# Seven products in two more down projections, with the weights' sums made in memory by GpSimd's transfers

## The chip, the core and the metric

One core of one Trainium2 chip runs the whole program. The metric is the device time of one execution in microseconds; the median of several runs is given. TensorE multiplies (with weight loads beside), VectorE (DVE) and ScalarE (ACT) do elementwise work, GpSimd (POOL) some more of it, and SyncE (SP) issues the transfers.

## What is computed

One decoder layer on 576 tokens (512 of a prompt, 64 of samples), width 1024: a token mixer (gated linear attention and retention, four heads each), cross attention into a memory of 256 tokens, and a squared-ReLU MLP with 4096 hidden columns. Around each stands a pair of RMS norms. The part that the change touches, and the norms at the start:

```python
def rmsnorm(x, g):
    xf = x.astype(jnp.float32)
    y = xf * lax.rsqrt(jnp.mean(xf * xf, axis=-1, keepdims=True) + EPS)
    return (y * g.astype(jnp.float32)).astype(x.dtype)
...
    m, s_gla_new, s_ret_new = mixer_block(rmsnorm(x, g_pre_mix), ...)
    x = x + rmsnorm(m, g_post_mix)
    x = x + rmsnorm(cross_attn(rmsnorm(x, g_pre_xa), mem_k, mem_v, w_xq, w_xo), g_post_xa)
    hf = rmsnorm(x, g_pre_ffn)
    x = x + rmsnorm(jnp.square(jax.nn.relu(hf @ w_up)) @ w_down, g_post_ffn)
```

## The kernel before

**Products.** Activations lie transposed, columns of the model on partitions, 576 tokens in two halves of NH = 288. Every product of float32 is made of three matmuls of a faster type (fp32r), high by high, low by high, high by low (`mm3`, lines 251 to 253). So each operand is split into two tiles: ScalarE casts the high part (line 93) and VectorE subtracts it for the low part (line 94). `gemm_m` makes 128 columns by 576 tokens over the inner dimension of 1024 from one tile of weights.

**Weights.** A list `plan` holds all weight tiles in the order of use. `wfetch` has SP load the next one (512 KB) into one of six ring buffers `wraw` (line 180), `wsplit` splits it, `wnext` hands the pair on and keeps loads and splits ahead.

**MLP.** The hidden columns come in four groups g of 1024. Group 0 is made plainly, 384 matmuls up and 384 down. The hidden columns of groups 1 to 3 are made by `sevenfold`: a 2 x 2 block product (halves of the inner dimension and of the columns, with the tokens' halves) from seven products instead of eight, A11, S1, S2, A12, S3, S4 and A22, each 12 matmuls, in four blocks b; S1 to S4 multiply sums of blocks. The activations' sums are made once (`sums_f`, in `fsh`, `fsl`), and the weights' sums by VectorE, four subtractions of 512 columns a block (`minus`, line 213, in `begin`). In the down projection groups 1 and 2 are plain: eight calls of `gemm_m`, added into `y3`. The last group's down projection is the end of the kernel.

**What sets the order.** The code is written in one stream; `side` holds generators of work that `tick` advances between products, and a scheduler of the language then orders the instructions of each engine, by its own estimates of when operands are there. Each engine runs its list in order.

**The start.** SP loads the memory `mf`, the first weights `in_w_xk`, and the two halves of x (`xf`). TensorE makes the keys of the memory from its unnormalized columns and the norm is applied behind. For a norm, VectorE and ScalarE add squares up (`sq`, `ss`, `mss`, lines 349 to 353, last sum line 322), TensorE adds over partitions (line 324), VectorE scales (`ms`, line 326), GpSimd raises to the power -1/2 (`rs`, line 333), VectorE puts it on a diagonal (`dg`, line 335) and TensorE spreads it (line 342). Then VectorE scales x to `xn`, ScalarE casts `xh`, and GpSimd subtracts for `xl` (line 98). `mst` (line 415) are the memory's keys on their way out.

**The mixer.** Eight units (head, branch) of about 60 us follow from 68 us on; GpSimd makes their head norms' `rs` (line 874), which TensorE's transposes (line 1016) wait for by way of VectorE.

Of the kernel before, what the change touches and what calls it, by code (L numbers as in the profile page):

```python
# [13 lines left out]
P = 128  # L14
KT = 8
# [43 lines left out]
def decoder_step(ctx, tc, xT, memT, ktc, vc, s_gla, s_ret, w_in, w_ga, w_a2, w_mix, w_xq, w_xk, w_xv, w_xo,  # L59
                 w_up, w_ups, w_down, vecs, cst, gam, y_out, mk_out, mv_out, sg_p, sr_p, sg_s, sr_s):  # L60
# [102 lines left out]
    def seven(w, b0):  # L163
        return [(w[b0 + b][:, kh], SEVEN) for b in range(4) for kh in range(2)]
# [18 lines left out]
    def wsplit():
        if units:
            units.pop(0)()
        elif raws:
            if raws[0][1] == SEVEN:
                begin()
                return
# [4 lines left out]
            pool = staying[-1] if mode == STAY else wp  # L194
            wh = pool.tile([P, 1024], F32R, name="wh")
            wl = pool.tile([P, 1024], F32R, name="wl")
            split(wh, wl, raw)
            ready.append((wh, wl))

    def halves(w):  # L200
        return w.rearrange("p (q n) -> p q n", q=2)

    def begin():


        while len(raws) < 2:
            wfetch()
        p0, p1 = (raws.pop(0)[0] for _ in range(2))
        t = wp.tile([P, 1024], F32, name="wraw", bufs=N_RAW)
        q0, q1, qt = halves(p0), halves(p1), halves(t)  # L210

        def minus(out, a, b):
            nc.vector.tensor_tensor(out=out, in0=a, in1=b, op=ALU.subtract)

        def ring(raw):
            wh = wp.tile([P, 1024], F32R, name="wh")
            wl = wp.tile([P, 1024], F32R, name="wl")
            split(wh, wl, raw)
            ready.append((wh, wl))

        def own(raw, o, n):
            w = wq[0][:, o:o + n], wq[0][:, o + n:o + 2 * n]
            split(*w, raw)
            ready.append(w)

        def unit_a():
            ring(p0)
            wfetch()

        units.extend([unit_a, lambda: ring(t), lambda: own(p1, 0, 1024),  # L230
                      lambda: minus(q1[:, 0], q1[:, 0], qt[:, 0]), lambda: own(q1[:, 0], 2048, 512)])
# [41 lines left out]
    def sevenfold(x, p1, p5, u2, c11, c22, c12, c21):  # L273
# [374 lines left out]
    xnp = ctx.enter_context(tc.tile_pool(name="xnp", bufs=2))  # L648
# [4 lines left out]
    def add(out, a, b, op=ALU.add):  # L653
        nc.vector.tensor_tensor(out=out, in0=a, in1=b, op=op)  # L654

    def sums_f():

        for j in range(4):
# [5 lines left out]
            add(c2[:, 1], c2[:, 0], c2[:, 1])  # L664
            add(c2[:, 0], c1[:, 0], c2[:, 0], ALU.subtract)
            add(c1[:, 0], c2[:, 1], c1[:, 0], ALU.subtract)
            add(c1[:, 1], c1[:, 1], c1[:, 0], ALU.subtract)
            yield
            split(fsh[:, 2:4, j], fsl[:, 2:4, j], c2)
            split(fsh[:, 0:2, j], fsl[:, 0:2, j], c1)  # L670
            yield

    FQ = {"A11": (fh, fl, 0), "A12": (fh, fl, 1), "A22": (fh, fl, 3),
# [748 lines left out]
```

## Time and profile before

| | us |
|---|---|
| median of 3 runs | 1200.71 (1199.32 to 1202.62) |
| the profiled execution, whole | 1199.37 |
| its span in the trace | 1197.6 |
| start until the mixer's first product | 67.6 |
| mixer, cross attention | 68 to 572, 572 to 806 |
| MLP and last norm | 806 to 1197.6 |

The page gives for each engine how long it was busy in the span. The tables of stretches give the same for parts of it, with the clock that TensorE was granted and the share of time in which the 16 transfer engines were busy. In the groups by line, "busy, mean ns of one | idle before, releaser" says how long such instructions took and what the engine had waited for just before them. A timeline's row is: start, duration, engine, line, operation, output <- inputs, shape; in brackets the idle time ahead and who ended it.

### The profile page before, as it was taken

The numbers are of one execution on the slowest core, as the hardware profiler recorded it, in microseconds if no ns is written. First come the engines' busy times: TensorE is split into PE (matmuls) and PEld (weight loads), VectorE is DVE, ScalarE is ACT, GpSimd is POOL, SyncE is SP. The second block draws the span as 40 slices with busy tenths as digits, with TensorE's granted clock in tenths as the row PEclk, the third lists the DMA queues.
The fourth block names the chain that finished last, engine by engine and source line by source line (L and its number), as shares of the span: only waits on it lengthen the run. The fifth ranks groups of instructions, "written<-read, shape, count | busy, mean of one in ns | idle before, by whom it ended". The sixth has DMA issues, their size and how long they took to land.

```text
span 1197.6 us, 21977 instructions
## 1 busy us (share of the span) xinstructions
PE 1168.7 (98%) x9006; PEld 1137.6 (95%) x9006; DVE 746.6 (62%) x1332; ACT 563.3 (47%) x992; POOL 155.1 (13%) x165
## 2 busy tenths in 40 slices
PE   8899999999999999999999999999999999999995
PEld 8899999999999999999999878989999999999995
DVE  6745757465747565757868545686937546456565
ACT  5534546442445244524555434566527416515652
POOL 0522213122312222221001000000000000000000
PEclk9899999999999999999999999999999999999998
DMA  8772424242324332322644677753223223321631
GB/s 290 228 244 79 129 79 128 72 144 72 127 89 128 89 128 79 121 88 93 213 134 138 215 260 232 235 177 123 88 71 107 88 71 105 107 71 57 215 110 60
DMA packets 65621, 158.37 MB, mean 132 GB/s; under 512 B 5648, under 2 KB 34448, under 8 KB 65392
## 3 DMA queue, kind: packets, MB, share of 16 engines
q1 hardware_dynamic: 65520, 156.96, 41.0%
q8 instruction: 71, 1.16, 0.4%
q14 instruction: 30, 0.25, 0.1%
HBM read 140.68 MB, written 16.25 MB: 131 GB/s over the span
## 4 chain that ended last, share of the span: by engine, by line
PE 90%; DVE 4%; DMA 3%; issue 1%; POOL 1%; ACT 1%; SPq 0%; POOLq 0%; DVEq 0%; ACTq 0%
PE psg L251 22%; PE psg L252 22%; PE psg L253 22%; PE psa L281 6%; PE psg L281 3%; PE psa L251 2%; PE pso L281 2%; PE psa L252 1%; PE psa L253 1%; PE pso L1241 1%; DMA xf<-in_xT 1%; PE psa L1084 1%; DVE wl L94 1%; PE pso L1079 1%; DVE res L526 1%
## 5 line engine op out<-in xcount | busy, mean ns | idle before, releaser
L251 PE MATMUL psg<-xh,wh 128*128 128x288 f32 x1296 | 385.5, 298 | 0.0
L252 PE MATMUL psg<-xh,wl 128*128 128x288 f32 x1296 | 381.9, 295 | 0.8 <-DVE wl L94 0.8
L253 PE MATMUL psg<-xl,wh 128*128 128x288 f32 x1296 | 381.9, 295 | 0.0
L94 DVE TENSOR_TENSOR wl<-wraw,wh 128x1024 fp32r<-128x1024 f32 x197 | 243.4, 1236 | 89.3 <-ACT wh L93 88.5
L93 ACT CAST wh<-wraw 128x1024 fp32r<-128x1024 f32 x197 | 207.0, 1051 | 187.6 <-PE psg L253 108.2
L251 PEld LDWEIGHTS psg<-xh,wh 128*128 128x128 f32 x1296 | 243.2, 188 | 2.2 <-issue 0.8
L252 PEld LDWEIGHTS psg<-xh,wl 128*128 128x128 f32 x1296 | 243.3, 188 | 1.1 <-DVE wl L94 1.0
L253 PEld LDWEIGHTS psg<-xl,wh 128*128 128x128 f32 x1296 | 243.1, 188 | 0.1
L251 PE MATMUL psg<-hh,wh 128*128 128x288 f32 x512 | 151.2, 296 | 0.7 <-DVE y L760 0.6
L252 PE MATMUL psg<-hh,wl 128*128 128x288 f32 x512 | 151.0, 295 | 0.3 <-DVE wl L94 0.3
L253 PE MATMUL psg<-hl,wh 128*128 128x288 f32 x512 | 151.0, 295 | 0.0
L251 PEld LDWEIGHTS psg<-hh,wh 128*128 128x128 f32 x512 | 96.2, 188 | 1.6 <-issue 1.1
L252 PEld LDWEIGHTS psg<-hh,wl 128*128 128x128 f32 x512 | 96.1, 188 | 0.6 <-DVE wl L94 0.6
L253 PEld LDWEIGHTS psg<-hl,wh 128*128 128x128 f32 x512 | 96.2, 188 | 0.0
L333 POOL TENSOR_TENSOR rs<-ms,mhalf 96x3 f32<-96x3 f32 (+1 forms) x11 | 11.0, 998 | 521.5 <-DVE ms L326 521.5
L942 ACT COPY vt<-psg 128x512 f32<-128x512 f32 x16 | 9.4, 586 | 77.8 <-PE psg L253 77.8
L874 POOL TENSOR_TENSOR rs<-mv,mhalf 128x1 f32<-128x1 f32 x48 | 29.7, 619 | 112.7 <-DVE mv L869 64.6
L944 DVE COPY vd<-psg 128x128 f32<-128x128 f32 x32 | 7.8, 285 | 55.8 <-ACT vt L942 55.8
L251 PE MATMUL psg<-bh,wh 128*128 128x288 f32 x128 | 38.4, 300 | 1.6 <-ACT wh L93 1.1
L654 DVE TENSOR_TENSOR y<-psg,y 128x576 f32<-128x576 f32 x16 | 12.1, 756 | 44.2 <-PE psg L253 44.2
L252 PE MATMUL psg<-fh,wl 128*128 128x288 f32 x128 | 38.2, 298 | 0.9 <-DVE wl L94 0.9
L253 PE MATMUL psg<-fl,wh 128*128 128x288 f32 x128 | 37.9, 296 | 0.6 <-DVE fl L94 0.6
(324 smaller groups left out, 2406.2 us busy)
## 6 DMA issues: line engine op xcount, KB each, us to landing
wraw<-in_w_in SPq DMA_DIRECT2D x64, 512.0 KB, 3.7
wraw<-in_w_down SPq DMA_DIRECT2D x38, 512.0 KB, 3.7
wraw<-in_w_ups SPq DMA_DIRECT2D x24, 512.0 KB, 3.6
wraw<-in_ktc SPq DMA_DIRECT2D x16, 512.0 KB, 5.0
wraw<-in_vc SPq DMA_DIRECT2D x16, 512.0 KB, 4.4
wraw<-in_w_xq SPq DMA_DIRECT2D x14, 512.0 KB, 3.9
wraw<-in_w_xo SPq DMA_DIRECT2D x14, 512.0 KB, 5.5
wraw<-in_w_up SPq DMA_DIRECT2D x14, 512.0 KB, 4.3
```

The lines of the kernel that those rows point to most:

```text
L93: nc.scalar.copy(hi, src)
L94: nc.vector.tensor_tensor(out=lo, in0=src, in1=f32(hi), op=ALU.subtract)
L251: nc.tensor.matmul(out, ah, bh, start=first, stop=False)
L252: nc.tensor.matmul(out, al, bh, start=False, stop=False)
L253: nc.tensor.matmul(out, ah, bl, start=False, stop=last)
L281: nc.tensor.matmul(out, s[:, q, k], m[:, k], start=first and k == i == 0, stop=k == 3 and i == 2, skip_group_check=True)
L526: nc.vector.tensor_tensor(out=res[:, kk, c], in0=y[:, kk], in1=rj, op=ALU.add)
L654: nc.vector.tensor_tensor(out=out, in0=a, in1=b, op=op)
L874: nc.gpsimd.tensor_tensor(out=rs[:t], in0=mv[:t], in1=mhalf[:t, 0:1], op=ALU.pow)
L1079: nc.tensor.matmul(so[32 * j:32 * j + 8, o], qsd[:, b * 8:b * 8 + 8], s0[:, j], start=False, stop=True, skip_group_check=True, tile_positi ...
L1084: nc.tensor.matmul(U[:, j * 256:(j + 1) * 256], kst[g][:, 2 * bp + j, :], vst[g], start=True, stop=True)
L1241: nc.tensor.matmul(acc[rows, :256], x(h), w[:, h], start=first, stop=last, skip_group_check=True, tile_position=(0, 32 * h))
```

## The change

The down projection of groups 1 and 2 is made by `sevenfold`, too: 336 matmuls instead of 384. The sums of hidden columns that it multiplies are made by `pairs` on VectorE, with the splits. The order of the products is new (A11, S1, S2, S4, S3, A12, A22; A12 second in a down stage's first block, `late`). VectorE no longer makes the weights' sums. GpSimd's transfers make them in memory (`t_sev`), for five stages, two blocks at a time: eight transfers of 512 KB for a pair of blocks, four that copy and four that add to what is there, 80 in all. `sums` issues them in the mixers, four calls in each unit, by the numbers in SUMS_AT and SUM_STEPS, each time behind a tiny copy `pace` on GpSimd that reads a tile just made. SP then loads the ring's tiles in two halves of 256 KB.

```diff
+SUMS_AT = (2, 5, 7, 10, 12, 15, 17, 20, 22, 25)
+SUM_STEPS = (0, 0, 1, 1, 2, 3, 4, 5)
...
+        for n in range(b0, b0 + 4):
+            g, i = n // 2, n % 2
+            b = [w_sev[q, n] for q in range(4)]
+            t1, t2, t4 = t_sev[g]
+            out += [((b[0], t1[i]), RING), ((t2[0, i], t2[1, i]), RING), ((b[2], b[3]), RING), ((t4[i],), LAST)]
...
     for g in range(1, 4):
-        plan += seven(w_ups, 4 * (g - 1))
-        plan += whole(w_down, 4 * g) + (rest(whole(w_down, 12), 0) if g == 3 else [])
+        plan += seven(8 * (g - 1))
+        plan += seven(8 * g - 4) if g < 3 else whole(w_down, 4) + rest(whole(w_down, 4), 0)
...
+        for n, (dst, src, plus) in zip(SUM_STEPS, (
+                (t1, b11, 0), (t2[1], b12, 0), (t1, b12, 1), (t2[1], b22, 1),
+                (t2[0], t1, 0), (t2[0], b22, 1), (t4, t2[0], 0), (t4, b21, 1))):
+            steps.setdefault(at + n, []).append((dst, src, plus))
...
+    def sums(after):
+
+        if clock[0] in steps:
+            nc.gpsimd.tensor_copy(pace, after)
+        for dst, src, plus in steps.pop(clock[0], ()):
+            nc.gpsimd.dma_start(out=dst, in_=src, max_dma_last_dim=8192, **({"accum_op": ALU.add} if plus else {}))
+        clock[0] += 1
...
+            if isinstance(src, tuple):
+                for i, t in enumerate(src):
+                    nc.sync.dma_start(out=raw[:, i * 512:(i + 1) * 512], in_=t)
...
-        minus(qt[:, 1], q1[:, 1], q0[:, 1])
-        minus(q0[:, 1], q0[:, 1], q0[:, 0])
-        minus(qt[:, 0], q1[:, 1], q0[:, 1])
...
         prod(acc, wa, 0, "A11", True)
-        p1(acc)
...
+        nc.scalar.copy(c1[:, 0], acc)
+        if late:
+            c11()
+        prod(c, wa, 1, "S1", True)
+        nc.scalar.copy(c2[:, 1], c)
+        wmore()
         wd = ready.pop(0)
...
         prod(acc, wc, 0, "S2", False)
-        wsplit()
-        u2(acc)
-        prod(b, wb, 0, "A12", True)
-        more()
-        c11(b)
+        nc.scalar.copy(c1[:, 1], acc)
+        wmore()
+        prod(c, wb, 1, "S4", False)
+        add(c1[:, 1], c, c1[:, 1], ALU.subtract)
         prod(acc, wc, 1, "S3", False)
...
+        add(c2[:, 1], c2[:, 1], acc, ALU.subtract)
+        done22()
+        wmore()
+        if not late:
+            c11()
+        done1()
+        wmore()
         prod(acc, wd, 0, "A22", False)
...
+    def pairs(c1, c2, sh, sl):
+
+        add(c2[:, 1], c2[:, 0], c2[:, 1], ALU.subtract)
+        add(c2[:, 0], c1[:, 0], c2[:, 0], ALU.subtract)
+        split(sh[:, 2:4], sl[:, 2:4], c2)
+        add(c1[:, 0], c2[:, 1], c1[:, 0], ALU.subtract)
+        add(c1[:, 1], c1[:, 1], c1[:, 0])
+        split(sh[:, 0:2], sl[:, 0:2], c1)
...
+            def done22():
+                relu2(c2[:, 1])
+                if not plain:
+                    split(fh[:, 2, b], fl[:, 2, b], c2[:, 1])
...
+            def done21(ps):
+                nc.scalar.copy(c2[:, 0], ps)
+                add(y[1], y[1], c2)
+
+            sevenfold(xh7, c1, c2, lambda: add(y[0], y[0], c1), lambda: None, done21, b == 0)
...
+            sums(kf[:, 511:512])
```

GpSimd's list at the start, before (`rs` and `xl` as above):

```order
L333 ISA
L333 TENSOR_TENSOR rs_244<-ms_242,mhalf_84 128x2
L333 TENSOR_TENSOR rs_329<-ms_327,mhalf_84 96x3
L98 TENSOR_TENSOR xl_112<-xn_369,xh_111 128x288
L98 TENSOR_TENSOR xl_112<-xn_373,xh_111 128x288
L98 TENSOR_TENSOR xl_112<-xn_377,xh_111 128x288
L98 TENSOR_TENSOR xl_112<-xn_411,xh_111 128x288
L98 TENSOR_TENSOR xl_112<-xn_415,xh_111 128x288
```

and now:

```order
L198 DMA t_sev00<-in_w_sev 64x2048
L198 DMA t_sev01<-in_w_sev 64x2048
L198 DMA t_sev00<-in_w_sev 64x2048
L198 DMA t_sev01<-in_w_sev 64x2048
L198 DMA t_sev01<-t_sev00 64x2048
L198 DMA t_sev10<-in_w_sev 64x2048
L333 ISA
L333 TENSOR_TENSOR rs_245<-ms_243,mhalf_84 128x2
L198 DMA t_sev01<-in_w_sev 64x2048
L333 TENSOR_TENSOR rs_330<-ms_328,mhalf_84 96x3
L198 DMA t_sev11<-in_w_sev 64x2048
L198 DMA t_sev02<-t_sev01 64x2048
```

Six transfers now stand ahead of the memory's rs, one more ahead of the rs of x's first half and two more ahead of the first xl.

VectorE's list at the start, from the memory norm's `ms` on, before:

```order
L326 TENSOR_SCALAR ms_242<-psa_238 128x2
L335 TENSOR_TENSOR dg_246<-idn_81,rs_244 128x256
L397 COPY mrs_152<-rs_244 128x2
L94 TENSOR_TENSOR wl_340<-wraw_169,wh_339 128x1024
L353 TENSOR_TENSOR ss_233<-ss_233,sq_235 128x576
L415 TENSOR_TENSOR mst_289<-psg_164,mbc_153 128x512
L415 TENSOR_TENSOR mst_333<-psg_249,mbc_153 128x512
L353 TENSOR_TENSOR ss_233<-ss_233,sq_280 128x576
L94 TENSOR_TENSOR wl_384<-wraw_203,wh_383 128x1024
L353 TENSOR_TENSOR ss_233<-ss_233,sq_283 128x576
L322 TENSOR_TENSOR ss_233<-ss_233 128x288
```

and now:

```order
L326 TENSOR_SCALAR ms_243<-psa_239 128x2
L97 TENSOR_TENSOR wl_341<-wraw_170,wh_340 128x1024
L353 TENSOR_TENSOR ss_234<-ss_234,sq_236 128x576
L353 TENSOR_TENSOR ss_234<-ss_234,sq_281 128x576
L97 TENSOR_TENSOR wl_385<-wraw_204,wh_384 128x1024
L353 TENSOR_TENSOR ss_234<-ss_234,sq_284 128x576
L322 TENSOR_TENSOR ss_234<-ss_234 128x288
L335 TENSOR_TENSOR dg_247<-idn_81,rs_245 128x256
L397 COPY mrs_153<-rs_245 128x2
L326 TENSOR_SCALAR ms_328<-psa_323 96x3
L415 TENSOR_TENSOR mst_290<-psg_165,mbc_154 128x512
L415 TENSOR_TENSOR mst_334<-psg_250,mbc_154 128x512
```

The memory norm's dg and mrs stand behind the whole sum of squares of x's first half, and the two mst behind that.

TensorE's list around the product with dg (line 342), before:

```order
L253 MATMUL psg_249<-ml_119,wh_205 128x256
L251 MATMUL psg_249<-mh_118,wh_252 128x256
L252 MATMUL psg_249<-mh_118,wl_253 128x256
L342 MATMUL psa_286<-dg_246,idn_81 128x256
L253 MATMUL psg_249<-ml_119,wh_252 128x256
L251 MATMUL psg_249<-mh_118,wh_252 128x256
```

and now (`mm3` has moved to lines 247 to 249):

```order
L247 MATMUL psg_250<-mh_119,wh_253 128x256
L248 MATMUL psg_250<-mh_119,wl_254 128x256
L249 MATMUL psg_250<-ml_120,wh_253 128x256
L342 MATMUL psa_287<-dg_247,idn_81 128x256
L324 MATMUL psa_323<-idn_81,ss_234 96x1 x3
L247 MATMUL psg_337<-mh_119,wh_295 128x256
```

The product stands 22 matmuls later, behind the last of the second pair of key tiles, with the sum over partitions of x's first half right behind it.

TensorE's list where a group's hidden columns end and its down projection begins, before (`hh`, `hl` are the hidden columns' parts), and then now (`ha` the parts of two blocks, `hh`, `hl` the sums):

```order
L251 MATMUL psg_11305<-hh_10799,wh_11228 128x288
L252 MATMUL psg_11305<-hh_10799,wl_11229 128x288
L251 MATMUL psg_11361<-hh_10799,wh_11301 128x288
L252 MATMUL psg_11361<-hh_10799,wl_11302 128x288
L253 MATMUL psg_11361<-hl_10800,wh_11301 128x288
L251 MATMUL psg_11361<-hh_10799,wh_11301 128x288
L253 MATMUL psg_11305<-hl_10800,wh_11228 128x288
```

```order
L277 MATMUL psa_11493<-ha_10916,wh_11404 128x288
L277 MATMUL psa_11493<-ha_10916,wl_11405 128x288
L277 MATMUL pso_11494<-ha_10916,wh_11465 128x288
L277 MATMUL pso_11494<-ha_10916,wl_11466 128x288
L277 MATMUL psg_11495<-hh_10914,wh_11404 128x288
L277 MATMUL psg_11495<-hh_10914,wl_11405 128x288
L277 MATMUL psg_11495<-hl_10915,wh_11404 128x288
L277 MATMUL psg_11495<-hh_10914,wh_11404 128x288
L277 MATMUL psa_11493<-ha_10916,wh_11404 128x288
L277 MATMUL pso_11494<-ha_10916,wh_11465 128x288
```

Before, two tiles' products alternate over the first of the inner dimension; now those of A11, A12 and S1 do.

## Rows read from the trace of the kernel before

**Rows 1.** The page's first part: busy us, share of the span, instructions.

```profile
PE 1168.7 (98%) x9006; PEld 1137.6 (95%) x9006; DVE 746.6 (62%) x1332; ACT 563.3 (47%) x992; POOL 155.1 (13%) x165
```

**Rows 2.** Stretches: length, busy PE, PEld, DVE, ACT, POOL; clock, DMA share, GB/s.

```profile
0.00:20.00 20.00, 16.11 (x97) 15.24 (x98) 11.66 (x20) 12.45 (x20) 0.90 (x5) 0.91 0.88 320
...
40.00:50.00 10.00, 6.95 (x50) 6.54 (x49) 8.72 (x10) 5.74 (x10) 5.79 (x5) 0.84 0.92 282
50.00:60.00 10.00, 10.00 (x70) 9.71 (x69) 5.21 (x8) 4.57 (x9) 4.91 (x5) 0.82 0.49 159
...
70.00:290.00 220.00, 219.25 (x1704) 215.45 (x1703) 129.43 (x289) 95.52 (x184) 47.47 (x50) 1.00 0.36 114
...
891.80:936.90 45.10, 45.10 (x339) 44.86 (x338) 29.68 (x39) 30.11 (x51) 0.00 (x0) 1.00 0.37 117
936.90:988.05 51.15, 51.15 (x386) 51.01 (x386) 23.97 (x28) 11.65 (x15) 0.00 (x0) 1.00 0.20 62
...
1033.10:1084.30 51.20, 51.20 (x387) 51.06 (x386) 23.97 (x28) 11.68 (x15) 0.00 (x0) 1.00 0.21 63
```

**Rows 3.** Groups by form in a hidden stage, 891.8 to 936.9 us.

```profile
L93 ACT CAST wh<-wraw 128x1024 fp32r<-128x1024 f32 x9 | 9.5, 1054 | 10.8 <-PE psa L281 10.8
...
L93 ACT CAST hh<-hr 128x576 fp32r<-128x576 f32 x6 | 3.7, 667 | 0.0
...
L727 ACT COPY hr<-psa 128x288 f32<-128x288 f32 x4 | 1.6, 399 | 0.8 <-PE psa L281 0.8
...
L94 DVE TENSOR_TENSOR wl<-wraw,wh 128x1024 fp32r<-128x1024 f32 x9 | 11.0, 1224 | 8.4 <-ACT wh L93 8.4
L94 DVE TENSOR_TENSOR hl<-hr,hh 128x576 fp32r<-128x576 f32 x6 | 4.3, 756 | 2.4 <-ACT hh L93 2.4
L213 DVE TENSOR_TENSOR wraw<-wraw 128x512 f32<-128x512 f32 x6 | 4.1, 686 | 0.1
...
L654 DVE TENSOR_TENSOR hr<-psa,hr 128x288 f32<-128x288 f32 x4 | 1.8, 458 | 3.9 <-PE psa L281 3.9
```

**Rows 4.** TensorE's timeline at the start.

```profile
19.96 0.28 PE L251 MATMUL psg<-mh,wh 128*128 128x256 f32 x1
20.08 0.28 PE L252 MATMUL psg<-mh,wl 128*128 128x256 f32 x1
20.52 0.70 PE L342 MATMUL psa<-dg,idn 128*128 128x256 f32 x2 [0.16 <-DVE dg L335]
...
47.80 1.12 PE L324 MATMUL psa<-idn,ss 128*96 128x1 f32 x6 [2.96 <-DVE ss L322]
...
67.56 0.30 PE L251 MATMUL psg<-xh,wh 128*128 128x288 f32 x1
```

**Rows 5.** VectorE's timeline at the start.

```profile
20.03 0.43 DVE L335 TENSOR_TENSOR dg<-idn,rs 128x256 f32<-128x256 f32 x1 [0.82 <-POOL rs L333]
...
23.05 1.52 DVE L415 TENSOR_TENSOR mst<-psg,mbc 128x512 f32<-128x512 f32 x2
...
27.07 0.46 DVE L322 TENSOR_TENSOR ss<-ss 128x288 f32<-128x288 f32 x1
```

**Rows 6.** GpSimd's timeline at the start.

```profile
33.28 2.54 POOL L98 TENSOR_TENSOR xl<-xn,xh 128x288 fp32r<-128x288 f32 x2 [2.98 <-ACT xh L97]
...
49.27 0.84 POOL L333 TENSOR_TENSOR rs<-ms,mhalf 96x3 f32<-96x3 f32 x1 [3.76 <-DVE ms L326]
...
64.56 1.44 POOL L98 TENSOR_TENSOR xl<-xn,xh 128x288 fp32r<-128x288 f32 x1 [0.32 <-ACT xh L97]
```

**Rows 7.** The page's transfers: count, KB each, median us from issue to landing.

```profile
wraw<-in_w_ups SPq DMA_DIRECT2D x24, 512.0 KB, 3.6
...
wraw<-in_w_xk SPq DMA_DIRECT2D x8, 512.0 KB, 7.6
```

**Rows 8.** Timeline of the mixer's first unit, GpSimd and TensorE.

```profile
134.06 0.55 POOL L874 TENSOR_TENSOR rs<-mv,mhalf 128x1 f32<-128x1 f32 x1 [1.00 <-DVE mv L869]
...
136.34 0.38 PE L1016 MATMUL psa<-idn,on 128*128 128x128 f32 x2
```

More of the change, by code (lines that the diff above doesn't have):

```diff
@@ L161, in decoder_step, with seven @@
     plan += rest(whole(w_xo), 0)
-    def seven(w, b0):
-        return [(w[b0 + b][:, kh], SEVEN) for b in range(4) for kh in range(2)]
+    def seven(b0):
+        out = []
+        for n in range(b0, b0 + 4):
[3 more added lines that the diff above has]
+            out += [((b[0], t1[i]), RING), ((t2[0, i], t2[1, i]), RING), ((b[2], b[3]), RING), ((t4[i],), LAST)]
+        return out
     plan += whole(w_up) + rest(whole(w_up), 0) + whole(w_down)
@@ L170, in decoder_step @@
+    clock = [0]
+    pace = perm.tile([P, 1], F32, name="pace")
+    def sums(after):
[4 more added lines that the diff above has]
+        clock[0] += 1
     raws, ready, staying = [], [], []
-    wq = []
-    units = []
+    wdp = []
     def wfetch():
-        if plan and sum(m == SEVEN for _, m in raws) < 2:
+        if plan:
@@ L181, in wfetch @@
             raws.append((raw, mode))
     def wsplit():
[L184 to L189, printed above, removed]
+        if raws:
             raw, mode = raws.pop(0)
@@ L193, in wsplit, with wmore @@
                 return
[L194 to L197, printed above, removed]
+            n = 512 if mode == LAST else 1024
+            pool = wdp[0] if mode == LAST else staying[-1] if mode == STAY else wp
+            wh = pool.tile([P, n], F32R, name="wh")
+            wl = pool.tile([P, n], F32R, name="wl")
+            split(wh, wl, raw[:, :n])
             ready.append((wh, wl))
[L200 to L206, printed above, removed]
+    def wmore():
+        while plan and len(raws) < N_RAW - 1:
             wfetch()
[L208 to L231, printed above, removed]
-        minus(qt[:, 1], q1[:, 1], q0[:, 1])
-        minus(q0[:, 1], q0[:, 1], q0[:, 0])
-        minus(qt[:, 0], q1[:, 1], q0[:, 1])
-        wfetch()
+        wsplit()
     def wnext(n=P):
         while sum(len(r) == 2 for r in ready) < 2 and (raws or plan):
-            while not units and plan and len(raws) + sum(len(r) == 1 for r in ready) < N_RAW - 1:
-                n0 = len(raws)
+            while plan and len(raws) + sum(len(r) == 1 for r in ready) < N_RAW - 1:
                 wfetch()
-                if len(raws) == n0:
-                    break
-            if not raws and not units:
+            if not raws:
                 break
@@ L663, in sums_f @@
             yield
[L664 to L667, printed above, removed]
+            pairs(c1, c2, fsh[:, :, j], fsl[:, :, j])
             yield
[L669 to L673, printed above, removed]
-          "S2": (fsh, fsl, 0), "S4": (fsh, fsl, 1), "S3": (fsh, fsl, 2), "S1": (fsh, fsl, 3)}
+    SQ = {"S2": 0, "S4": 1, "S3": 2, "S1": 3}
     def xf7(n):
-        h, l, q = FQ[n]
-        return h[:, q], l[:, q]
+        return (fsh[:, SQ[n]], fsl[:, SQ[n]]) if n in SQ else tuple(
+            t[:, {"A11": 0, "A12": 1, "A22": 3}[n]] for t in (fh, fl))
     y3 = None
@@ L683, in decoder_step, with xh7 @@
         hl = acta.tile([P, 4, 4, NH], F32R, name="hl", tag="xl")
+        plain = g in (0, 3)
+        ha = None if plain else biga.tile([P, 2, 2, 4, NH], F32R, name="ha", tag="biga")
+        def xh7(n):
+            if n in SQ:
+                return hh[:, SQ[n]], hl[:, SQ[n]]
+            return (fh[:, 2], fl[:, 2]) if n == "A22" else (ha[:, 0, n == "A12"], ha[:, 1, n == "A12"])
         if g == 0:
@@ L739, in decoder_step, with done21 @@
+        if plain:
+            break
+        for b in range(4):
+            c1, c2 = (hp.tile([P, 2, NH], F32, name="hr") for _ in range(2))
+            y = [y3[:, 2 * b:2 * b + 2, hc(half)] for half in range(2)]
+            def done21(ps):
+                nc.scalar.copy(c2[:, 0], ps)
+                add(y[1], y[1], c2)
+            sevenfold(xh7, c1, c2, lambda: add(y[0], y[0], c1), lambda: None, done21, b == 0)
     res2 = fsp.tile([P, KT, NT], F32, name="res2", tag="fsh")
@@ L1122, in unit @@
                 tick()
+            sums(G[:, 1, NT - 1:])
             for m in range(2):
@@ L1128, in unit @@
                 tick()
+            sums(G[:, 1, NT - 1:])
             def finish():
```

104 lines of the change are left out of this document (49 added, 55 removed).

## The prediction

> **What bounds the kernel now.** I read the busy shares first: TensorE is busy 1168.7 of the 1197.6 us span and no other engine passes 62% [rows 1]. A change pays, then, by taking matmuls away or by closing the few holes in TensorE's row. The table of stretches comes next [rows 2]: in the stretch 70 to 290 and in the middle groups of the MLP TensorE is busy practically all the time at granted clock 1.00 (the higher of its two levels, 2.4 GHz). The holes are at the start: between 40 and 50 us it works 6.95 us of 10, and the granted clock of that stretch and of the next is 0.84 and 0.82, though TensorE is busy all of the next. There the DMA share also matters: 0.88 of all 16 engines in the first 20 us, against 0.36 later. I then read the groups of one hidden stage, since its helpers get new work, and last the timelines of the start, because the order of the changed program is most altered there.
>
> **The saving.** A plain down stage has 384 matmuls and takes 51.15 and 51.20 us [rows 2]: 0.1332 us each. By seven products it has 4 blocks of 7 x 12 = 336. The up stage that is built so now takes 45.10 us; 336 x 0.1332 is 44.8, and I take 44.9. Two stages: 2 x (51.15 - 44.9) = **12.5 us** less, all on the path, as TensorE does not pause in either kind. The bounds are 12.1 (at 45.10) and 12.8.
>
> **Helpers in the hidden stages.** The weights' sums, four passes of 0.686 us in each of 4 blocks, 2.7 us a block, leave VectorE's queue; six of the sixteen lie in the stage that the rows show, the others in the stage before it [rows 3]. In groups 1 and 2 a block now gets four sums of 288 columns, 4 x 0.458 = 1.8 us, and 288 + 576 more columns to split, at 0.756 for 576 some 1.2 us on VectorE and, at 0.667, 1.1 us on ScalarE. So VectorE's work for a stage hardly grows (+0.3 a block), but more of it must be done inside the stage: a block has 3 x 1.224 + 0.7 of weight splits, 7 x 0.458 of sums and 3.5 x 0.756 of splits, 10.2 us, 41 for four, less the last block's 2 to 3 that fall into the next stage: at most 38 of 45 us, where 29.68 are busy now. ScalarE comes to 30.11 + 4 x 1.1 = 34.5. Neither becomes the bound by its sum. What tightens is a deadline: a product lasts 12 x 0.1332 = 1.6 us, and in the new order S4 adds to the bank whose S1 must have been copied out first, with only S2 between (three products now). ScalarE's copy of S1 takes 0.399 us, and behind a weight cast of 1.054 us that just started it ends 1.45 us after S1's last matmul: just inside 1.6. In the new down stages the helpers have less to do, and where hidden ends and down begins, TensorE's order runs A11 and A12 over three quarters of the inner dimension before it needs the last block's result, so that seam should cost 0 to 0.3 us. For seams and deadlines I take **+1.5 us**, from 0 (TensorE's rows show no pause in the stages now) to 5 (twenty blocks by 0.25).
>
> **GpSimd's transfers.** Eighty transfers of 512 KB from memory to memory, half of which add, are new. No row of before shows one. What does each hold GpSimd for? Between nothing and one of its ordinary operations of 2.54/2 = 1.27 us [rows 6]; 80 of them are at most 102 us beside 155.1 of work on an engine that is busy 13%. How long until one has landed? Loads of the same size take 3.6 us in the quiet MLP and 7.6 us at the start [rows 7]; I take 5 to 7.6 for a copy there, and for one that adds from the same (one pass) to twice that (it reads its target, too): 5 to 15, and take 9. What room do they take? At 320 GB/s for a share of 0.88, all 16 engines move 364 GB/s, so 512 KB fill them for 1.44 us, and twice that where it adds. Eighty fill them for 40 x 1.44 + 40 x 2.88 = 173 us. The order shows that the hold does not hold the early ones: 33 stand ahead of the first pace copy, six ahead of the first rs, and all 80 by about the fourth of eight mixer units. From 70 to 290 us 64% of 220 us is free, 141 us, so the mixer can take nearly all of it; the ring's six tiles cover slower loads. There I charge **+0.5 us** (0 to 3) for GpSimd being late with an rs that TensorE waits for.
>
> **The start.** Three things move. First, in VectorE's queue the memory norm's dg stood right behind its rs and is now behind the whole sum of squares of x's first half. In before, dg runs at 20.03 us and that sum ends at 27.07 + 0.46 = 27.53 [rows 5]. Ahead of it VectorE now has dg and the two mst passes (1.52) less; but squares and sums take turns on one buffer, so I regain 1.1 of this and not all: 26.4, with dg 0.43 behind it 26.9. Second, six transfers of GpSimd, four plain and two that add, come into the first stretch: 4 x 1.44 + 2 x 2.88 = 11.5 us of full engines, while 0.12 of 20 us is free. Shared out they would push x's first half by anything from 0 to 9 us; I take 2.5, since the two that add must wait for copies to land and so fall late. That makes the product of dg ready at 29.4. Third, TensorE's order has that product (L342) 22 matmuls later than now. It now starts at 20.52, after a wait of 0.16, and matmuls there start 0.12 us apart [rows 4]; so TensorE comes to it at 20.36 + 22 x 0.12 = 23.0 and then waits **6.4 us**, both PSUM buffers of the projection being full. Against this stands the wait of 2.96 us for the sum of x's second half at 47.80, which I count as gone: the order has the second half's loads ahead of the stores that they stood behind, and its squares earlier. Behind the hole at 40 to 50 the clock cost 10 x 0.16 + 10 x 0.18 = 3.4 us [rows 2]; I let the new hole cost the same, so the clock's cost moves and does not change. 6.4 - 3.0 = **+3.4 us**. The bounds: loads not pushed and VectorE's 2.1 us regained in full give a wait of 2.9 and so 0, and -1.5 if half of the clock's cost goes with the smaller hole; loads pushed by 7 give +8.
>
> By a rule of the Trainium skill (page "DMA: Bandwidth & Descriptors", section "Anatomy of one DMA — SWDGE (gpsimd) path") such a transfer takes about 2.0 us and its bytes by 436 GB/s, an estimate of 3.2 us for 512 KB. With it a copy would land sooner than any row of before here and the sum would be about 2 us lower. No transfer of GpSimd is in this trace to try it on.
>
> **Sum.** 1197.6 - 12.5 + 1.5 + 3.4 + 0.5 = 1190.5 us of span. The profiled run took 1199.37, 1.8 more than its span, so 1192.3 by that run, 7.1 less. The median of the runs is 1200.71, 1.34 above it: **1193.6 us**. With every term at its low bound it is 1186, and with the start and the mixer at their high ones 1201.
>
> **Rivals.** (A) The forecast, 1186 to 1196: chance 0.56.
>
> (B) The start is filled. The loads of x and of the first weights are pushed by 7 us and not 2.5, as the first 20 us have only 2.4 us of free engines for 11.5 us of work. For it: the share of 0.88 [rows 2]. Against it: only two of the six can go before a landing. The wait at L342 is then 11: 1193.6 + 4.6 = 1198. Chance 0.12. The Trainium skill (page "DMA: Bandwidth & Descriptors", section "Issuing engines are not separate DMA queues") states that transfers started by SP, ScalarE and GpSimd run on the same 16 engines and interleave, which would be this rival's mechanism; this trace has only SP's queue beside instruction loads and cannot show it.
>
> (C) Slower than before: GpSimd's own queue. Its transfers wait for each other's landing, and its norm work stands behind these waits. Copy, add, copy, add must have landed in turn before the first xl can pass, and one that adds, issued after two xl, before the rs of x's second half. In before the first xl is at 33.28, that rs at 49.27, the last xl ends at 66.0 and TensorE starts the mixer's first product at 67.56 [rows 4, 6]; with my start that is 71, which leaves 5 us. With copies of 7.6 us and adds of 12 the chain stands at 1 + 7.6 + 12 + 7.6 + 12 = 40, the xl pair at 43, and the next add lands at 55: 5.4 late, as much as the slack. So it decides at 12 us for each adding transfer; every microsecond above counts three times. At 17 us it is 15 us of stall, 1193.6 + 15 = 1209. For it: three reads and writes in place of two, at the fullest time. Against it: 9 is my value, from loads of 7.6. Chance 0.14.
>
> (D) The deadline of 1.45 in 1.6 us is missed in the hidden blocks: 8 blocks of groups 1 and 2, by 1 us each, where VectorE's fuller queue also holds the splits: 1193.6 - 1.5 + 8 = 1200. Chance 0.10.
>
> (E) GpSimd is late in the mixer. The rs at 134.06 lasts 0.55 and the product behind it starts at 136.34 [rows 8], so 1.7 us with VectorE's and TensorE's steps between: a transfer's wait of 2 to 3 us in front of it costs 1 us or two, in some of 8 units: 1199. Chance 0.08.
>
> That the hold does not do what it says is no rival but certain by the order, and is in the start's term.
>
> **How the numbers follow.** The measurement can tell about 0.3%, 3.6 us, from no change: faster is below 1197.1, slower above 1204.3. Faster: A's 0.56, 0.04 of B, and 0.02 of D and E: 0.62. Slower: C and 0.02 of B and E: 0.16. The rest, 0.22, is the same. The range takes in A, B, D and E and the mild part of C: 1186 to 1204, which leaves out C's greater part and little else.
>
> **What would show it.** Two down stages of 44.8 to 45.2 us, without pauses above 0.1 us on TensorE; a wait of TensorE for dg of L335 near 23 to 29 us and none of 3 us near 48; the mixer's first product at 71 instead of 67.56; VectorE and ScalarE near 37 and 35 us in a hidden stage. I am wrong if the first xl on GpSimd ends its wait on a transfer and the first mixer product comes after 76 (C), if that wait at L342 is over 9 us (B), or if products in the hidden stages wait for ScalarE's copy (D).

## The result and the profile after

The changed kernel takes 1207.42 us (median of 4 runs, 1205.92 to 1208.96) against 1200.77 before: a ratio of 1.0052, 95% interval 1.0039 to 1.0065. It is slower, where I forecast 1193.6 and a range that ended at 1204. Its profiled execution took 1208.4 us with a span of 1206.7, 9.1 us more than before.

The page of the changed kernel: busy time by engine, the strip of the transfer engines in 40 slices, and the queues (packets, MB, share of 16 engines).

```profile
PE 1165.2 (97%) x8910; PEld 1132.9 (94%) x8910; DVE 760.9 (63%) x1372; ACT 596.0 (49%) x1068; POOL 211.8 (18%) x274
...
DMA  9999899999442424232365577655433455555732
...
q1 hardware_dynamic: 79920, 172.69, 43.9%
q0 software_dynamic: 6400, 41.95, 13.9%
```

TensorE has 96 matmuls less, 12.8 us of work at 0.1332 each, but is busy only 3.5 us less [rows 1], and it is idle for 41.5 us instead of 28.9. So it waits more, and part of its work runs slower. The strip says when: with GpSimd's queue (q0, new) the transfer engines are full in the first ten slices, 0 to 300 us. The stretches of the changed kernel, columns as in [rows 2]:

```profile
0.00:20.00 20.00, 12.55 (x68) 11.63 (x68) 7.36 (x14) 9.11 (x16) 4.12 (x10) 0.91 0.91 280
20.00:40.00 20.00, 13.04 (x69) 12.28 (x70) 11.81 (x18) 7.90 (x11) 3.46 (x5) 0.76 1.04 376
...
96.00:102.00 6.00, 6.00 (x25) 6.00 (x26) 1.78 (x2) 0.75 (x1) 0.21 (x1) 0.50 1.00 372
...
913.40:958.20 44.80, 44.80 (x338) 44.80 (x337) 33.59 (x52) 33.88 (x62) 0.00 (x0) 1.00 0.46 147
958.20:1003.40 45.20, 45.20 (x336) 44.66 (x335) 30.17 (x43) 23.68 (x39) 0.00 (x0) 1.00 0.51 164
1003.40:1048.40 45.00, 45.00 (x340) 45.00 (x339) 35.41 (x55) 33.16 (x62) 0.00 (x0) 1.00 0.52 164
1048.40:1093.60 45.20, 45.20 (x336) 44.66 (x336) 30.19 (x42) 23.71 (x39) 0.00 (x0) 1.00 0.52 164
```

The last four are hidden and down stages of groups 1 and 2: the down stages take 45.2 us instead of 51.2 [rows 2], without a pause in either kind. The first two are the start: 68 and 69 matmuls in 20 us each, where the kernel before had 97 in the first [rows 2]. TensorE's timeline of the changed kernel, the rows that answer to [rows 4] with the waits before them, the mixer's first transposes (121.23), and the first product after the mixer:

```profile
10.25 0.58 PE L247 MATMUL psg<-mh,wh 128*128 128x256 f32 x1 [4.32 <-ACT mh L386]
...
36.01 0.70 PE L342 MATMUL psa<-dg,idn 128*128 128x256 f32 x2 [3.89 <-DVE dg L335]
...
79.65 0.30 PE L247 MATMUL psg<-xh,wh 128*128 128x288 f32 x1
...
95.87 0.61 PE L247 MATMUL psg<-xh,wh 128*128 128x288 f32 x1 [3.33 <-DVE ga L829]
...
121.23 0.27 PE L979 MATMUL psa<-idn,kf 128*128 128x128 f32 x1
...
592.89 0.38 PE L247 MATMUL psg<-bh,wh 128*128 128x288 f32 x1
```

and the last two of these in the kernel before:

```profile
102.74 0.27 PE L957 MATMUL psa<-idn,kf 128*128 128x128 f32 x1
...
572.29 0.38 PE L251 MATMUL psg<-bh,wh 128*128 128x288 f32 x1
```

The account of the 9.1 us, changed kernel against before, by the same products in both: +12.1 at the mixer's first product (79.65 against 67.56), +18.5 at the mixer's first transposes (121.23 against 102.74), +20.6 at its end, +21.8 at the MLP's first product (806.03 against 784.25); then the MLP and the tail give 12.7 back. So the start lost 18.5, the mixer 2.1, the cross attention 1.2.

Up to the first transposes both kernels run the same 692 matmuls. The stretch in the changed kernel and, below it, in the one before:

```profile
0.00:121.23 121.23, 101.53 (x692) 98.64 (x693) 63.97 (x92) 48.86 (x76) 45.70 (x56) 0.90 0.98 311
```

```profile
0.00:102.74 102.74, 95.07 (x692) 92.69 (x693) 62.38 (x92) 48.11 (x76) 30.11 (x28) 0.95 0.70 232
```

Of the 18.5 us, then, 12.0 are waits (TensorE is idle for 19.7 us instead of 7.7), and 6.5 are busy time that grew at a granted clock of 0.90 instead of 0.95 on average.

The loads at the start, from the transfers issued in the first 40 us of the changed kernel (count, KB each, median us to landing):

```profile
wraw<-in_w_xk SPq DMA_DIRECT2D x8, 512.0 KB, 12.3
t_sev<-in_w_sev POOLq DMA_DIRECT2D x7, 512.0 KB, 7.9
...
xf<-in_xT SPq DMA_DIRECT2D x8, 288.0 KB, 12.7
mf<-in_memT SPq DMA_DIRECT2D x4, 256.0 KB, 7.9
```

w_xk took 7.6 us before [rows 7]. GpSimd's own timeline at the start of the changed kernel:

```profile
8.29 0.83 POOL L198 DMA_DIRECT2D t_sev<-in_w_sev  x1 [5.71 <-DMA t_sev<-in_w_sev]
...
26.93 0.72 POOL L333 TENSOR_TENSOR rs<-ms,mhalf 128x2 f32<-128x2 f32 x1 [9.12 <-DVE ms L326]
...
37.42 0.87 POOL L333 TENSOR_TENSOR rs<-ms,mhalf 96x3 f32<-96x3 f32 x1 [8.95 <-DVE ms L326]
...
45.41 1.69 POOL L101 TENSOR_TENSOR xl<-xn,xh 128x288 fp32r<-128x288 f32 x1 [6.07 <-ACT xh L100]
```

It does wait for landings (8.29), but the first two rs and the first xl find it idle and wait for VectorE and ScalarE, which wait for data. The third rs, at 62.48, comes 2.9 us after its ms: two xl and the issue of one transfer stand ahead of it, no landing, and TensorE waits 0.88 us for what follows from it. The second loss, at 92 to 102 us, is a store's: ScalarE's cast a2s uses memory that an out_mv store still reads.

```profile
82.76 0.55 SPq L448 DMA_DIRECT2D out_mv<-mst  x1
...
93.70 0.62 ACT L824 CAST a2s<-t 96x512 fp32r<-96x512 f32 x1 [10.96 <-DMA out_mv<-mst]
```

These stores land in 10.8 us there (median of three) and in 4.4 in the kernel before, where ScalarE was idle for 6.58 us ahead of the same cast and TensorE did not wait. Now TensorE waits 3.33 us, and its granted clock is then 0.50 (the lower level, 1.2 GHz) for 6 us (the row 96 to 102 above), which costs 3 more.

### The profile page after: what moved, and what is told of

The parts are those of the page before. It is cut to its first block, busy times and chain, and to the rows that moved or that the text cites. A ratio compares the mean times of both kernels' runs of the same rounds, so it can differ in the third digit from the quotient of the medians.

```text
span 1206.7 us, 22343 instructions
## 1 busy us (share of the span) xinstructions
PE 1165.2 (97%) x8910; PEld 1132.9 (94%) x8910; DVE 760.9 (63%) x1372; ACT 596.0 (49%) x1068; POOL 211.8 (18%) x274
## 4 chain that ended last, share of the span: by engine, by line
PE 87%; DMA 5%; DVE 4%; ACT 1%; issue 1%; POOL 0%; SPq 0%; POOLq 0%; DVEq 0%; ACTq 0%
PE psg L247 19%; PE psg L248 19%; PE psg L249 19%; PE psa L277 11%; PE psg L277 5%; PE pso L277 3%; PE psa L247 2%; PE psa L248 1%; PE psa L249 1%; DMA wraw<-in_w_xk 1%; DMA out_mk<-mst 1%; PE pso L1265 1%; DMA wraw<-in_w_xo 1%; DVE wl L97 1%; DMA out_sgs<-sn 1%
## 5 line engine op out<-in xcount | busy, mean ns | idle before, releaser
L97 DVE TENSOR_TENSOR wl<-wraw,wh 128x1024 fp32r<-128x1024 f32 x237 | 283.7, 1198 | 120.5 <-ACT wh L96 117.1
L96 ACT CAST wh<-wraw 128x1024 fp32r<-128x1024 f32 x237 | 240.1, 1014 | 139.5 <-PE psg L249 47.5
L247 PE MATMUL psg<-hh,wh 128*128 128x288 f32 x256 | 76.1, 298 | 0.7 <-DVE y L780 0.6
L248 PE MATMUL psg<-hh,wl 128*128 128x288 f32 x256 | 75.4, 295 | 0.3 <-DVE wl L97 0.3
L249 PE MATMUL psg<-hl,wh 128*128 128x288 f32 x256 | 75.4, 295 | 0.0
L198 POOL DMA_DIRECT2D t_sev<-in_w_sev x60 | 43.9, 742 | 31.4 <-DMA t_sev<-t_sev 16.6
L247 PEld LDWEIGHTS psg<-hh,wh 128*128 128x128 f32 x256 | 48.1, 188 | 1.2 <-issue 1.1
L248 PEld LDWEIGHTS psg<-hh,wl 128*128 128x128 f32 x256 | 48.0, 188 | 0.6 <-DVE wl L97 0.6
L249 PEld LDWEIGHTS psg<-hl,wh 128*128 128x128 f32 x256 | 48.0, 188 | 0.2 <-DVE hl L97 0.2
L353 DVE TENSOR_TENSOR ss<-ss,sq 128x576 f32<-128x576 f32 x34 | 25.6, 753 | 20.9 <-ACT sq L352 20.9
## 6 DMA issues: line engine op xcount, KB each, us to landing
wraw<-in_w_in SPq DMA_DIRECT2D x64, 512.0 KB, 4.9
t_sev<-in_w_sev POOLq DMA_DIRECT2D x60, 512.0 KB, 8.2
wraw<-in_w_down SPq DMA_DIRECT2D x22, 512.0 KB, 3.7
t_sev<-t_sev POOLq DMA_DIRECT2D x20, 512.0 KB, 6.6
wraw<-in_ktc SPq DMA_DIRECT2D x16, 512.0 KB, 5.5
wraw<-in_vc SPq DMA_DIRECT2D x16, 512.0 KB, 4.6
```

Source lines behind the costliest of these rows:

```text
L96: nc.scalar.copy(hi, src)
L97: nc.vector.tensor_tensor(out=lo, in0=src, in1=f32(hi), op=ALU.subtract)
L198: nc.gpsimd.dma_start(out=dst, in_=src, max_dma_last_dim=8192, **({"accum_op": ALU.add} if plus else {}))
L247: nc.tensor.matmul(out, ah, bh, start=first, stop=False)
L248: nc.tensor.matmul(out, al, bh, start=False, stop=False)
L249: nc.tensor.matmul(out, ah, bl, start=False, stop=last)
```

## The experiments

**Held.** An edge for the scheduler that the transfers of a step follow their pace copy in GpSimd's list. All engines' lists at the start are then those of the kernel before.

```diff
-            nc.gpsimd.tensor_copy(pace, after)
-        for dst, src, plus in steps.pop(clock[0], ()):
-            nc.gpsimd.dma_start(...)
+            p = nc.gpsimd.tensor_copy(pace, after)
+            with tc.issue_after(p.ins):
+                for dst, src, plus in steps.pop(clock[0]):
+                    nc.gpsimd.dma_start(...)
```

> The changed kernel with one thing added: each group of GpSimd's transfers is queued behind its pace copy, so none starts before the mixer's first unit (about 110 us); the lists of all engines at the start are then those of the kernel before, and all 80 transfers still run. If the start's loss comes from the early transfers, by whatever way: the first mixer product at 67 to 68 us (79.65 in the changed kernel) and a time of 1187 to 1191 us. If the transfers' own load slows the mixer wherever they stand: the first product at 68 but a loss of 4 to 8 us between 100 and 500 us, 1193 to 1197. If the loss at the start has another cause than the transfers: no change, 1205 to 1209.

Measured: 1196.59 us (ratio to before 0.9948, 0.9927 to 0.9969). TensorE's timeline, the mixer's first product and the first behind the mixer:

```profile
66.29 0.30 PE L248 MATMUL psg<-xh,wh 128*128 128x288 f32 x1
...
578.30 0.38 PE L248 MATMUL psg<-bh,wh 128*128 128x288 f32 x1
```

The start's loss is gone, all of it: 66.3, and 101.5 at the first transposes, even 1.3 ahead of before. So the early transfers, with the order that they bring, are its cause. But the mixer now loses 7.3 us (512.0 between the two rows against 504.7 before), the size that the second theory had for the transfers' load. That theory is tried further down.

**Small transfers.** All lists as in the changed kernel, each transfer cut to 1/32; the ring reads plain weights, the weights' sums are left out.

```diff
-            nc.gpsimd.dma_start(out=dst, in_=src, max_dma_last_dim=8192, ...)
+            nc.gpsimd.dma_start(out=dst[:, :4], in_=src[:, :4], max_dma_last_dim=8192, ...)
```

> The changed kernel with every list of GpSimd, VectorE, ScalarE and TensorE as it is, all 80 transfers in their places with their waits, but each moves 16 KB instead of 512 KB, and the ring loads plain weights of the same size (the weights' sums are left out). Traffic theory: nearly all of the start's loss is gone, first mixer product at 68 to 71, 1188 to 1192 us. Order theory (VectorE's late dg and TensorE's late product with it cost by themselves, as my start's term had it, 6 us of wait and the clock): first product at 73 to 77, 1195 to 1201. Queue theory (GpSimd's waits for landings): small transfers land in 2 to 3 us, so most of the loss would go here, too; it is told apart by the rows of GpSimd: its xl and rs would have to wait for transfers in the changed kernel.

Measured: 1192.61 us (0.9925, 0.9905 to 0.9946). TensorE's timeline:

```profile
28.00 1.22 PE L342 MATMUL psa<-dg,idn 128*128 128x256 f32 x2 [4.59 <-DVE dg L335]
...
68.96 0.30 PE L247 MATMUL psg<-xh,wh 128*128 128x288 f32 x1
...
104.16 0.27 PE L979 MATMUL psa<-idn,kf 128*128 128x128 f32 x1
```

The moved order has its wait of 4.6 us at dg, but the first product is only 2.7 us later than in the held kernel: other waits of the start are gone for it. The second loss is gone, too: of the 18.5 us, 1.4 are left at the first transposes. The other 10.7 of the 13.4 us between the held and the changed kernel's first product come with the bytes. The lists are the same here, but GpSimd's waits on landings are shorter (4.5 us for a transfer of 16 KB against 7.9), so this run alone doesn't tell full engines from these waits; GpSimd's rows above and the dead copies below do.

**Copies only.** The 40 transfers that add only copy; the sums are left out.

```diff
-            nc.gpsimd.dma_start(..., **({"accum_op": ALU.add} if plus else {}))
+            nc.gpsimd.dma_start(...)
```

> The changed kernel with all lists as they are, but the 40 transfers that add only copy (the weights' sums are left out). If adding fills the engines for twice a copy's time, the traffic before the mixer falls by a third: first mixer product at 74 to 77 and 1200 to 1204 us. If an adding transfer costs what a copy costs: 79 to 80 and 1206 to 1209.

Measured: 1197.97 us (0.9971, 0.9955 to 0.9988), the mixer's first product at 75.37. The page's queue row:

```profile
q0 software_dynamic: 6400, 41.95, 10.3%
```

80 copies took 0.103 x 1194.7 = 123 us of all engines, 1.54 each. In the changed kernel it was 0.139 x 1206.7 = 168, so one that adds takes (168 - 40 x 1.54) / 40 = 2.65. Both are near my 1.44 and 2.88. The first product came early by 4.3 us and the second stall is gone, too (111.0 at the first transposes): the adding itself cost some 10 of the 18.5 us. The time lies below my band of 1200 to 1204.

**Dead copies.** The held kernel with 6, 2 or 12 plain copies at the head of GpSimd's list that nothing waits for.

```diff
+    for n in range(6):
+        nc.gpsimd.dma_start(out=t_dead[n], in_=w_sev[n % 4, 2 * (n // 4):2 * (n // 4) + 2], max_dma_last_dim=8192)
     raws, ready, staying = [], [], []
```

> The held kernel with six dead copies of 512 KB put at the very start of GpSimd's list, which nothing waits for; VectorE's and TensorE's lists at the start then come out as in the changed kernel. 6 x 1.44 = 8.6 us of full engines. Traffic theory: first mixer product 5 to 9 us later than in the held kernel, 1193 to 1198. Queue theory: nothing waits on GpSimd, so within 2 us of the held kernel or of the kernel with small transfers.

> The held kernel with two dead copies of 512 KB at the very start of GpSimd's list, and VectorE's list at the start as in the kernel before: traffic alone, with no order moved. A copy filled the engines for 1.54 us (10.3% of 1194.7 us for 80 copies), so 3.1 us. If each microsecond of the engines at the start costs one of TensorE: first mixer product at 69 to 70 us (66.3 held), 1197 to 1200. If the free share of the first 67 us (some 20%) takes them up: 66 to 67, 1194 to 1197. If six copies cost 12 us mostly by the order that came with them: under 1 us here.

> The same with twelve dead copies, 18.5 us of full engines. One for one: first mixer product at 84 to 88 us (66.3 held, 78.4 with six), 1213 to 1218. If there is a limit, the six having delayed the first loads once and for all: 78 to 81, 1206 to 1210.

Measured: 1207.71 us with six (1.0054, 1.0033 to 1.0076), 1202.78 with two (1.0017, 0.9994 to 1.0039; its runs spread from 1196 to 1206), 1220.91 with twelve (1.0172, 1.0145 to 1.0198). TensorE's timeline, the mixer's first product, with two, six and twelve in turn:

```profile
67.62 0.30 PE L250 MATMUL psg<-xh,wh 128*128 128x288 f32 x1
```

```profile
78.36 0.29 PE L250 MATMUL psg<-xh,wh 128*128 128x288 f32 x1
```

```profile
92.45 0.29 PE L250 MATMUL psg<-xh,wh 128*128 128x288 f32 x1
```

and with six, of the transfers issued in the first 40 us (count, KB each, median us to landing), the first weights' and the memory's:

```profile
wraw<-in_w_xk SPq DMA_DIRECT2D x8, 512.0 KB, 14.0
...
mf<-in_memT SPq DMA_DIRECT2D x4, 256.0 KB, 12.7
```

From 66.3 the first product moves by 1.3, 12.1 and 26.2 us, for 3.1, 9.2 and 18.5 us of engines. Of the 12.1, about 2.7 can be the order, which moves with six and not with two. So traffic alone, with nothing on GpSimd waiting, does what the changed kernel shows up to the first product; the queue theory's limit of 2 us is passed by far.

With twelve the order moves once more: in VectorE's list the memory norm's dg stands behind the sum of x's second half, too, and TensorE waits 12.0 us for it, where it waits 4.6 with six. VectorE and TensorE with twelve:

```profile
51.31 0.46 DVE L325 TENSOR_TENSOR ss<-ss 128x288 f32<-128x288 f32 x1
51.69 0.42 DVE L338 TENSOR_TENSOR dg<-idn,rs 128x256 f32<-128x256 f32 x1
```

```profile
52.16 1.22 PE L345 MATMUL psa<-dg,idn 128*128 128x256 f32 x2 [12.03 <-DVE dg L338]
```

So the 26.2 us are no price of traffic alone. With two the time is 6.2 us above the held kernel's, and the start explains 1.3 of it: the mixer takes 4.0 us more, most of it where TensorE waits behind a state's store that is still under way (the case is told under One hold):

```profile
391.70 0.41 PE L1041 MATMUL psa<-idn,on 128*128 128x128 f32 x2 [2.22 <-DVE ag L889]
```

Neither of my rules of proportion holds: two copies were half hidden, six cost about what they fill. The changed kernel's transfers, strung out by their waits, cost less for their size: 37% of the engines' time in the first 70 us, 26 us, moved the first product by 10.7 beyond the order. So the place of a transfer among the first loads counts beside its bytes; a law for it I can't give.

**Small transfers, held.** The two edits above together, to find where the held kernel loses in the mixer.

> The held kernel with all its lists as they are, but each of the 80 transfers moves 16 KB and the ring loads plain weights (the weights' sums are left out). It asks why the held kernel, level with the kernel before until the mixer starts (first product 66.3 against 67.6), comes out of the mixer 6.0 us behind it. Traffic theory (stores and loads of the mixer take longer beside the transfers): the mixer's loss falls to 1 us or less, 1185 to 1189 us. Queue theory (GpSimd's issuing, waiting and the moved instructions around it delay what TensorE needs): 5 to 7 us of loss stay, 1191 to 1195.

Measured: 1195.34 us (0.9945, 0.9930 to 0.9960). First product and end of the mixer:

```profile
66.59 0.30 PE L248 MATMUL psg<-xh,wh 128*128 128x288 f32 x1
...
340.25 0.37 PE L248 MATMUL psg<-xh,wh 128*128 128x288 f32 x1 [0.61 <-DVE qs L942]
...
578.25 0.38 PE L248 MATMUL psg<-bh,wh 128*128 128x288 f32 x1
```

511.7 us between first and last, as with the full transfers (512.0): most of the held kernel's loss in the mixer is not traffic. The stretch from the first transposes to the end of the mixer, here and then in the kernel before:

```profile
102.48:578.25 475.77, 473.39 (x3672) 460.24 (x3671) 304.91 (x685) 209.08 (x424) 172.63 (x222) 1.00 0.34 104
```

```profile
102.74:572.29 469.55, 468.80 (x3673) 459.06 (x3671) 294.58 (x685) 209.63 (x424) 107.56 (x113) 1.00 0.33 103
```

Short waits as the one at 340 are 1.6 us of the loss (2.4 us idle against 0.8). In 4.6 us TensorE counts as busy with the same work, at a granted clock of 1.00. The lists of the mixer were made anew around the held steps; which instruction's place costs most, and why the busy time is longer, I have not settled.

**One hold.** All 80 follow the first pace copy alone.

```diff
             p = nc.gpsimd.tensor_copy(pace, after)
-            with tc.issue_after(p.ins):
+            first.append(p.ins)
+            with tc.issue_after(first[0]):
```

> The changed kernel with all 80 transfers queued behind the first pace copy alone, about 110 us, and free after that, so they run as densely as they did in the changed kernel, only 100 us later. The changed kernel lost 2 us in the mixer with its dense transfers up to 300 us, the held one 7 with its spread ones. If the spread holds are what costs in the mixer: first product at 66 to 67, 2 to 3 us of loss in the mixer, 1189 to 1192. If it is the transfers' traffic wherever it stands in the mixer: 6 to 8 us of loss, 1193 to 1197.

Measured: 1193.89 us (0.9933, 0.9917 to 0.9950), better than both kernels. The mixer (66.27 to 576.79) still loses 5.8 us. Most of that is one wait, and this wait is traffic. VectorE's and TensorE's timelines, and a stretch just behind:

```profile
253.71 0.69 DVE L1117 TENSOR_TENSOR sn<-s,psa 128x512 f32<-128x512 f32 x1 [4.16 <-DMA out_sgs<-sn]
254.32 0.48 DVE L903 TENSOR_SCALAR on<-psa,rs 128x256 f32<-128x256 f32 x1
...
254.94 0.41 PE L1041 MATMUL psa<-idn,on 128*128 128x128 f32 x2 [2.01 <-DVE on L903]
```

```profile
256.00:259.50 3.50, 3.50 (x18) 3.50 (x17) 3.04 (x12) 2.21 (x5) 3.48 (x5) 0.51 0.72 218
```

A state's store was still under way, sn (the new state) waited for its buffer, and TensorE's transpose waited for the instruction behind sn. That cost 2.0 us, and the granted clock of 0.51 behind it 1.7 more. The 2.1 us that are left are what the changed kernel lost in the mixer and what my first theory had. So the spread of the holds may have cost the held kernel the rest; these runs do not show it.

**Plain down projections.** The kernel with one hold, with groups 1 and 2 of the down projection plain again; the 80 transfers still run.

```diff
-        plan += seven(8 * g - 4) if g < 3 else whole(w_down, 4) + rest(whole(w_down, 4), 0)
+        plan += whole(w_down, 4 * g) + (rest(whole(w_down, 12), 0) if g == 3 else [])
...
+        for k in range(KT):
+            y = h2(y3[:, k, :])
+            add(y, gemm_m(quarters(hh, hl), None), y)
+            tick()
```

> The kernel with one hold, but the down projections of groups 1 and 2 plain again as in the kernel before; all 80 transfers still run, though the sums of two stages are not read. If the seven products save what the two stages' rows say, 12.5 us more than with them: 1204 to 1208 us, 2 to 6 above the kernel before. If part of that saving is eaten by the helpers in the hidden stages (three product banks, fuller VectorE): 1200 to 1203.

Measured: 1203.68 us (1.0024, 1.0014 to 1.0035), against 0.9933 with the seven products: 0.9% or 11 us. Group 1's two stages:

```profile
898.90:943.60 44.70, 44.70 (x338) 44.70 (x337) 26.21 (x34) 31.18 (x56) 0.00 (x0) 1.00 0.49 153
943.60:994.80 51.20, 51.20 (x386) 51.04 (x385) 17.11 (x18) 10.78 (x14) 0.00 (x0) 1.00 0.29 93
```

The hidden stage takes the same 44.7 or 44.8 us with the fuller helpers and without, the down stage 6 us more. The median, 1203.7, lies on the edge of the two bands I had set (1200 to 1203, 1204 to 1208); the rows decide for nearly the whole saving: from the MLP's first product to the end it is 412.5 us here and 400.6 with the seven products, 11.9 less. Without the saving the 80 transfers are a small loss even when held, 0.24%.

## Why the prediction was wrong, step by step

**The saving was right.** Foreseen 12.5 us; from the MLP's first product to the last products of the last group's down projection the kernel before takes 784.25 to 1182.71, the changed one 806.03 to 1192.27, 12.2 less.

**The helpers were right, with cover to spare.** I had put 1.5 us for missed deadlines and found no pause in the stages. VectorE is busy 33.6 and 35.4 us in the hidden stages (at most 38 foreseen), ScalarE 33.9 and 33.2 (34.5). The sums that replace VectorE's subtractions have these rows, of the first hidden stage:

```profile
L315 DVE TENSOR_TENSOR hr<-hr 128x288 f32<-128x288 f32 x12 | 5.5, 456 | 1.8 <-ACT hr L728 1.6
L97 DVE TENSOR_TENSOR hl<-hr,hh 128x576 fp32r<-128x576 f32 x6 | 4.5, 752 | 0.0
```

**The transfers' prices were near.** 1.54 and 2.65 us of engines (1.44 and 2.88 foreseen); landing in 7.9 us in the first 40 (foreseen 5 to 7.6 for a copy, 9 for one that adds); 0.5 to 1.05 us of GpSimd each in the first 130 us (0 to 1.27). The Trainium skill (page "DMA: Bandwidth & Descriptors", section "Anatomy of one DMA — SWDGE (gpsimd) path") gave an estimate of 3.2 us to landing for 512 KB. The traces don't agree: 8.2 over the whole run for those from the weights, and even the transfers of 16 KB took 4.5 at the start. It would have made my forecast worse.

**The start is the step that failed.** I had +3.4 and it was +18.5. Within the term, the order's part was about right: the wait at dg was foreseen with 6.4 us and is 4.6 with small transfers, TensorE comes to it at 23.4 there where I had 23.0, and the net cost, foreseen as under 1 us without the push, is 1.4 against the kernel before. Two parts of the term were wrong.

The push of the loads, 2.5 us in my sum, measured 10.7 us at the mixer's first product. I counted the engines only for the first stretch, six transfers and 11.5 us, and then let the loads slip into the gaps. But the order that I had read shows 18 ahead of the last xl, and the engines were 0.88 full in the first 20 us and 0.79 in the first 70 without them; 26 us of GpSimd's queue came into these 70. With the full transfers TensorE came to dg's product at 36.0 - 3.9 = 32.1 us: it had lost time before, at 10.25 (4.32) and at the weights' splits, since the memory's and the first weights' loads, which I had not pushed at all, came late. And the pressure did not end with x: the stores of the memory's values, which I never priced, held ScalarE at 93.7 and cost 6.4 more with the clock.

The clock's cost, which I let move and not change, grew by 6.5 us; they are contained in these 10.7 and 6.4, and are over a third of the 18.5: TensorE's granted clock was 0.76 from 20 to 40 us, behind its waits at the weights' splits and at dg, and 0.50 from 96 to 102, behind the store's. The kernel before had 0.84 and 0.82 from 40 to 60 and 1.00 from there to its first transposes.

**The rivals.** B, the filled start, was the mechanism, at chance 0.12 and with a price of 4.6 us: the experiments with small and with dead transfers show it, and they show by far more. Its sign was badly chosen: the wait at L342 is 3.9 us and not over 9, as TensorE came late itself. The Trainium skill's rule (page "DMA: Bandwidth & Descriptors", section "Issuing engines are not separate DMA queues") that transfers of all engines share the 16 engines agrees with this: w_xk's loads take 12.3 us beside GpSimd's transfers and 7.6 without. C ended near the measured time (1209) for the wrong reason: the first one that adds, issued at 8.29, had landed by 16.8, 8.5 us later, where my limit was 12 us, and GpSimd was idle when the first two rs and the first xl came. D did not occur. E was small in the changed kernel, 2.1 us in the mixer with all else (0.5 foreseen). The held kernels lose 6 to 7 us there, but no run shows that to be E, a late rs. That the hold does not hold I had read rightly from the order and then priced only in part.

## What to carry to other kernels

An instruction without operands that tie it down goes where the scheduler finds room, and for a transfer that is the start; a pace instruction ahead of it in the code is no hold unless an edge says so, and the order shows it before any run. When new transfers come into a stretch whose engines are 0.8 to 0.9 full, count all of them up to the end of that stretch, and price each load and store that stands beside them, not only the one that ends last now. A wait costs more than its length where TensorE's clock falls behind it, so a new wait is not to be taken at its length alone. A hold makes the lists around it anew, and that is to be read in the same way.

## What the runs showed of the hardware

A transfer from memory to memory that adds takes the engines for 2.65 us where a copy takes 1.54 (512 KB). A GpSimd transfer of 16 KB lands in 4.5 us beside a busy start, where one of 512 KB takes 7.9. Six copies, 9.2 us of engines, ahead of the first loads raised the landing of w_xk's loads from 8.1 us (held kernel) to 14.0 and moved the first product of the mixer by 12.1 us, of which 2.7 can be the order. After the start's waits the same 692 matmuls took 101.5 us of busy time instead of 95.1, at a mean granted clock of 0.90 instead of 0.95.
